# Small retention products for two heads at once on row blocks, S5 outputs in the next input's burst, recurrent units in another order

## The chip, the cores and the metric

The kernel runs on one core of one Trainium2 chip, as one program. The metric is the device time of a run in microseconds (us); a result is the median of several runs. The engines are named as the profile names them: PE is TensorE (its matmuls; PEld are its weight loads), DVE is VectorE, ACT is ScalarE, POOL is GpSimd, SP is SyncE, which only issues DMAs here.

## The reference

One inference step of a two-layer decoder over 560 positions: 528 of a prompt (16 learned meta tokens ahead of 512) and 8 sequences of 4 sampled tokens, which bring their own states. `D_MODEL` is 1024, everything is float32. Each layer:

```
h = rmsnorm(x, g_pre_mix);  z = h @ w_in
u_a, x_b, g_b, q, k, v, g_c, gates = split(z)
y_a = s5_mixer(u_a)          # 48 groups of 16 channels, 64 complex states each;
                             # y = Re(C h) + D u; z = gelu(y); z * sigmoid(z @ w_glu + b)
y_b = rglru_mixer(x_b, g_b)  # width-4 convolution, gated linear recurrence, 768 channels
y_c = retention_mixer(q, k, v, g_c)   # 8 heads, dk 64, dv 128
m = sum of sigmoid(gate_i) * (y_i @ w_branch_i), i = a, b, c
x = x + rmsnorm(m @ w_out, g_post_mix)
h = rmsnorm(x, g_pre_ffn);  gf, uf = split(h @ ffn_w_up)
x = x + rmsnorm((gelu(causal_dwconv(gf)) * uf) @ ffn_w_down, g_post_ffn)
```

Retention works by chunks; for each head

```
scores = einsum('nd,md->nm', q, k) * decay
o      = einsum('nm,me->ne', scores, v) + einsum('nd,de->ne', q, s) * gamma**(n+1)
s_new  = gamma**C * s + einsum('md,me->de', k_dec, v)
```

and `o` is normalized over each head's 128 channels and multiplied by `silu(g_c)`. Outputs are y and the new states of all branches.

## The kernel before

**Columns and weights.** Channels lie on the 128 partitions, positions on the columns: a 1024-channel array is 8 tiles of 128x560, worked on in two halves of 280 columns (`HS`). Weights come in chunks (mostly 128x1024), in the order that `_order` writes out by hand; SP's queue brings each into a raw tile `wr`, ScalarE rounds it to a high part `wh` (fp32r), VectorE subtracts to get the low part `wl`. The same is done with the inputs (`hh`/`hl`, `yh`/`yl`, `fh`/`fl`, `zh`/`zl`). `half` then makes three products for each block of 128 rows, `wh*xh`, `wh*xl` and `wl*xh`, into a PSUM tile `pm`. These weight products are 16128 of TensorE's 19128 instructions. A chunk with 8 blocks is 24 products in each half.

**Small products.** In between stand the mixers' products in plain f32, in bursts, with PSUM tiles `px` (retention, recurrent unit, statistics; two buffers for each tag) and `pz` (S5; one buffer of two banks).

- `s5_gen` runs over n = 0 to 11 (four groups of channels each). For each n a side generator `ahead` makes the unit's weights (`build_B`, `build_C`, `pe_W`, `evac_W`, `build_T`: tiles `Bk`, `br`, `CA`, `Dt`, `W1`, tables `Tc`, `Ts`). Then: the input product (`pz<-V,W`, 16 matmuls on 64x64 tiles), VectorE's rotation and scan into `Hr`, `Hi`, and a step later in the loop `pe_Y(n-1)`: the output product of the unit before (`Hr,CA`, `Hi,CA` on 64x64 tiles, `V,Dt` on the full array), and `evac_Y(n-1)`. `bank(2)` lets only one of these products hold `pz` at a time; `zb` counts. `put_z` writes the outputs z to DRAM (`zd`), and they come back by 24 small loads at the start of the gated unit (`glu`).
- `ret_gen` treats a pair of heads (`hp` = 0 to 3): scores `kf*qf` of 112x112 for each of five chunks (four of the prompt, the fifth of 80 prompt and 32 sampled positions), `sc` by mask; chunk states `S`, a block-diagonal 128x256 tile for two heads; outputs `sc*v` and `S*qf` for both heads into one PSUM tile (`outs`); statistics and normalization; `km`, the sampled positions' keys spread over 8 sequences, times v for the new sample states `ss`; then the outputs are transposed and multiplied into `sg`, the gate's silu, and written to DRAM (`ycd`).

**Order of the work.** A Python planner writes out the program: `Paced` engines keep a model clock `clk`, and `pump`, called after half a unit of weight products, lets the side generators (`start`, `step`) go on when their results should be there and VectorE and ScalarE are not too far ahead (`DEEP`, `SHALLOW`). `finish` runs one to its end. Evacuations of `pm` wait in a list, and `flush` issues them. POOL's queue (`SQ`) takes all DMAs but the weights.

**A layer.** First the products of the u and k columns are made from an input that is not normalized yet. When the sums are there, `normalize` scales the tiles and splits them again, in place (the rewriting: eight `hh` copies and eight `hl` subtractions a half, in the second layer into the tiles named `fh`, `fl`); the products in between, among them v and the first gate `gc`, are scaled column by column with `rn`. Then come k, q, v, gc for each head pair, and between them `LPH` = (1, 1, 2, 2) of the six recurrent units (`xb`, `gb`). After the last pair: `NTC` = 6 of the eight `tc` gate chunks, the retention outputs back from DRAM and split in two (`load_split`, `yh`/`yl`), their projection (`bc`), the recurrent branch's (`tb`, `bb`), S5's gate (`ta`, `glu`) and projection (`ba`), `wo`, and the ConvFFN. In the last layer the halves are 272 and 276 columns.

Of the kernel before, what the change touches and what calls it, by code (L numbers as in the profile page):

```python
# [19 lines left out]
NT = 560  # L20
# [5 lines left out]
C = 112  # L26
MAGIC = 12582912.0
FGRP = (7, 7, 8)
LPH = (1, 1, 2, 2)
NTC = 6  # L30
# [13 lines left out]
_CST = [("ident", 128), ("cos", NT), ("sin", NT), ("causal", C), ("smask", C), ("rowf", 16), ("kdec", 16), ("kds", 64), ("g1", 16), ("g2", 16),  # L44
# [40 lines left out]
def tile_hybrid_decoder(ctx: ExitStack, tc: tile.TileContext, I, O, cfg=None):  # L85
# [123 lines left out]
    kdsT = cc("kds").rearrange("p (h s) -> p h s", h=8)  # L209
# [27 lines left out]
    st = {"raw": 0, "hi": 0, "next": 0, "pool": None, "ahead": 1, "land": 0.0, "paced": False, "shallow": cfg.get("sh0", 1.5), "norm": None}  # L237
# [76 lines left out]
    SLACK, DEEP, SHALLOW = cfg.get("slack", 0.6), cfg.get("deep", 6.0), cfg.get("shallow", 1.0)  # L314
# [27 lines left out]
    def pump():  # L342
# [10 lines left out]
        for s in sorted([s for s in side if not s[4]], key=lambda s: s[2]):  # L353
            if (s in side and s[1] <= clk["P"] and used["n"] + s[3] <= NG
                    and max(clk["V"], clk["A"]) - clk["P"] < (st["shallow"] if s[2] else DEEP)):
                step(s)
# [448 lines left out]
    def s5_gen(l, sp, p, ud, zd, qt):  # L805
# [104 lines left out]
        def pe_Y(n):  # L910
            py = z_ps()
            ca, d = CA[n % 2], Dt[n % 2]
            for j, x in enumerate(X[n]["H"]):
                for a, g, h in QUAD:
                    P.matmul(py[GS[g], a, 0:140], lhsT=ca[j][GS[h], a * 96 + 32:a * 96 + 96], rhs=k3(x)[GS[h], a, 0:140],
                             start=j == 0, stop=False)
            for a in range(2):
                P.matmul(py[:, a, 0:140], lhsT=d[:, a * 128:a * 128 + 128], rhs=V2(n, a), start=False, stop=True)
            X[n]["py"] = py

        def evac_Y(n):
            py = X[n]["py"]
            z = qt("z")
            for a in range(2):
                stt(z[:, a * 140:a * 140 + 140], V2(n, a), vv(l, "s5_d")[:, 2 * n + a:2 * n + a + 1],
                    py[:, a, 0:140], OP.mult, OP.add)
# [42 lines left out]
        for n in range(12):  # L969
# [7 lines left out]
            pz, W1 = z_ps(), x.pop("W1")  # L977
            for j in range(2):
                for a, g, h in QUAD:
                    P.matmul(pz[GS[h], a, j * 140:j * 140 + 140], lhsT=W1[GS[g], a, j * 64:j * 64 + 64], rhs=V2(n, a)[GS[g]],  # L980
                             start=True, stop=True)
# [31 lines left out]
            if n:  # L1013
                evac_Y(n - 1)
                zb["n"] -= 2
# [11 lines left out]
            for j, t in enumerate((hr, hi)):  # L1027
                A.copy(p["fin"][:, j * 24 + a0:j * 24 + a0 + 2], k3(t)[:, :, 140])
        yield 0
        pe_Y(11)  # L1030
# [134 lines left out]
    def ret_gen(l, hp, T, ycd, rp, before):  # L1165
# [77 lines left out]
        yield 2  # L1243
        ss = [slot("ss") for _ in range(2)]
        for h in range(2):
            SQ.dma_start(ss[h][:, :512], I["rets"][l, 2 * hp + h])
        S = rp["S"]
        fin = rp["fin"]
        for h in range(2):
            b = slice(64 * h, 64 * h + 64)  # L1250
            e = slice(h * 128, h * 128 + 128)
            V.tensor_copy(S[0][b, e], p0[b, 0:128])
            for c in range(1, 4):
                stt(S[c][b, e], S[c - 1][b, e], gCT[b, hp, 0:1], p0[b, c * 128:c * 128 + 128], OP.mult, OP.add)
            stt(fin[b, :], S[3][b, e], gCT[b, hp, 1:2], p4[b, :128], OP.mult, OP.add)
# [5 lines left out]
        def outs(c, po):  # L1261
            M = C if c < 4 else 80
            o0 = (c % 2) * 256
            for h in range(2):
                P.matmul(po[:C, o0 + h * 128:o0 + h * 128 + 128],
                         lhsT=(sc[h][:C, c * C:c * C + C] if c < 4 else sc[2][:C, h * C:h * C + C]), rhs=vs(c, h),
                         start=h == 0, stop=c == 0 and h == 1)
            if c:
                P.matmul(po[:M, o0:o0 + 256], lhsT=qf[:, c * C:c * C + M], rhs=S[c - 1], start=False, stop=c < 4)
            if c == 4:  # L1270
                for h in range(2):
                    for s in range(4):
                        P.matmul(po[:C, h * 128:h * 128 + 128], lhsT=qm[h][:, s * C:s * C + C], rhs=ss[h][:, s * 128:s * 128 + 128],
                                 start=False, stop=s == 3 and h == 1)

        def stats(c0, n, po):
            of.append(slot("of"))
            A.copy(of[-1][:C, :n * 256], po[:C, :n * 256])
            for i in range(2 * n):
                V.bn_stats(bn[:C, (c0 * 2 + i) * 6:(c0 * 2 + i) * 6 + 6], po[:C, i * 128:i * 128 + 128])  # L1280

        po, po2 = side_ps(), side_ps()
        outs(0, po)
        outs(1, po)
        outs(2, po2)
        outs(3, po2)
        yield 2
        stats(0, 2, po)
        stats(2, 2, po2)
        yield 0  # L1290
        po = side_ps()
        outs(4, po)
        drop(4)
        yield 3
        stats(4, 1, po)
        km = [slot("km") for _ in range(2)]
# [847 lines left out]
```

## Time and profile before

| | |
|---|---|
| three runs | 2315.74, 2313.77, 2318.67 us; median 2315.74 |
| the profiled execution | 2316.45 us, of which the span is 2314.7 |
| TensorE busy | 2258.6 us, 98% of the span, 19128 matmuls |
| VectorE, ScalarE, POOL busy | 69%, 39%, 14% |
| mean granted clock of TensorE | 0.992 |

The span is the time from the first to the last instruction in the trace, so the execution lies 1.75 us above it. Busy times of engines overlap; a busy TensorE says that a matmul is in it, not that it works at its peak. All instructions are recorded by one helper line (L134), so groups are told apart by their tiles: `pm<-yh,wl` is a product into `pm` of the tiles `yh` and `wl`.

### The profile page before, as it was taken

How to read it: one execution, taken by the hardware profiler on the slowest of the kernel's cores; microseconds unless marked ns; L12 is line 12 of the kernel's file. 1: busy time of each engine (PE TensorE's matmuls, PEld its weight loads, DVE VectorE, ACT ScalarE, POOL GpSimd, SP SyncE). 2: the span in 40 equal slices, each digit the busy share in tenths (PEclk: the TensorE clock that was granted, in tenths of full speed). 3: DMA queues.
4: the chain of work that ended last, by engine and by line, in shares of the span. 5: the costliest groups of instructions: out<-in, count | busy, mean ns of one | idle time of the engine just before them, and what ended most of it. 6: DMA issues, size and time to landing. Idle time of an engine off the chain costs nothing.

```text
span 2314.7 us, 47168 instructions
## 1 busy us (share of the span) xinstructions
PE 2258.6 (98%) x19128; PEld 2217.8 (96%) x19128; DVE 1596.6 (69%) x3817; ACT 906.5 (39%) x1965; POOL 334.1 (14%) x620
## 2 busy tenths in 40 slices
PE   8999999999999999999989999999999999999997
PEld 8999999999999999999989999999999999999996
DVE  7988799885456844546589888898864667364555
ACT  4344446332435433223333445363324354332231
POOL 3231122012010000000243221120111110000011
PEclk9999999999999999999999999999999999999998
DMA  5332333334243232222333332332333432323231
GB/s 177 119 122 82 99 121 103 114 111 121 83 127 126 99 106 86 84 92 83 114 118 100 123 102 92 120 129 87 118 105 95 139 123 96 113 79 95 83 118 46
DMA packets 77146, 245.91 MB, mean 106 GB/s; under 512 B 14272, under 2 KB 17216, under 8 KB 76928
## 3 DMA queue, kind: packets, MB, share of 16 engines
q1 hardware_dynamic: 52704, 175.98, 23.5%
q0 software_dynamic: 24224, 66.92, 9.5%
q8 instruction: 150, 2.46, 0.4%
q14 instruction: 68, 0.56, 0.1%
HBM read 208.23 MB, written 29.76 MB: 103 GB/s over the span
## 4 chain that ended last, share of the span: by engine, by line
PE 71%; DVE 9%; issue 4%; ACT 2%; DMA 2%; POOL 1%; POOLq 0%; DVEq 0%; ACTq 0%
PE pm L134 66%; PE px L134 3%; PE pz L134 2%; DVE wl L134 1%; DVE r L134 1%; ACT wh L134 1%; DMA y<-ycd 1%; DVE part L134 1%; DVE ga L134 1%; DVE sc L134 0%; DVE fo L134 0%; DVE sums L134 0%; POOL out_y L134 0%; DMA wr<-in_wa 0%; DVE cm L134 0%
## 5 line engine op out<-in xcount | busy, mean ns | idle before, releaser
L134 ACT CAST wh<-wr 128x1024 fp32r<-128x1024 f32 (+3 forms) x347 | 346.8, 1004 | 600.8 <-PE pm L134 473.8
L134 DVE TENSOR_TENSOR wl<-wr,wh 128x1024 fp32r<-128x1024 f32 (+3 forms) x347 | 403.6, 1165 | 186.8 <-ACT wh L134 186.5
L134 PE MATMUL pm<-fh,wh 128*128 128x280 f32 (+2 forms) x1632 | 482.1, 295 | 8.3 <-DVE part L134 3.6
L134 PE MATMUL pm<-mh,wh 128*128 128x280 f32 (+2 forms) x1664 | 484.1, 291 | 0.7 <-DVE gp L134 0.7
L134 PE MATMUL pm<-mh,wl 128*128 128x280 f32 (+2 forms) x1664 | 482.6, 290 | 0.0
L134 PE MATMUL pm<-ml,wh 128*128 128x280 f32 (+2 forms) x1664 | 481.9, 290 | 0.0
L134 PE MATMUL pm<-fl,wh 128*128 128x280 f32 (+2 forms) x1632 | 476.6, 292 | 2.7 <-DVE fl L134 2.7
L134 PE MATMUL pm<-fh,wl 128*128 128x280 f32 (+2 forms) x1632 | 475.6, 291 | 0.0
L134 PEld LDWEIGHTS pm<-fh,wh 128*128 128x128 f32 x1632 | 309.5, 190 | 13.4 <-ACT xi L134 3.8
L134 PEld LDWEIGHTS pm<-mh,wh 128*128 128x128 f32 x1664 | 312.8, 188 | 1.6 <-DVE gp L134 1.0
L134 PEld LDWEIGHTS pm<-ml,wh 128*128 128x128 f32 x1664 | 313.3, 188 | 0.3
L134 PEld LDWEIGHTS pm<-mh,wl 128*128 128x128 f32 x1664 | 313.2, 188 | 0.0
L134 PEld LDWEIGHTS pm<-fl,wh 128*128 128x128 f32 x1632 | 309.4, 190 | 3.4 <-DVE fl L134 3.1
L134 PEld LDWEIGHTS pm<-fh,wl 128*128 128x128 f32 x1632 | 309.6, 190 | 0.1
L134 PE MATMUL pm<-hh,wh 128*128 128x280 f32 x928 | 276.8, 298 | 8.5 <-ACT hh L134 6.4
L134 PE MATMUL pm<-hl,wh 128*128 128x280 f32 x928 | 272.5, 294 | 3.3 <-DVE hl L134 3.3
L134 PE MATMUL pm<-hh,wl 128*128 128x280 f32 x928 | 271.6, 293 | 1.0 <-DVE wl L134 1.0
L134 PEld LDWEIGHTS pm<-hh,wh 128*128 128x128 f32 x928 | 175.8, 189 | 12.8 <-ACT hh L134 8.7
L134 PEld LDWEIGHTS pm<-hl,wh 128*128 128x128 f32 x928 | 175.6, 189 | 4.7 <-DVE hl L134 4.5
L134 PEld LDWEIGHTS pm<-hh,wl 128*128 128x128 f32 x928 | 176.2, 190 | 1.3 <-DVE wl L134 1.3
L134 PE MATMUL pm<-yh,wh 128*128 128x280 f32 (+2 forms) x448 | 133.5, 298 | 3.3 <-ACT yh L134 3.3
L134 PE MATMUL pm<-yl,wh 128*128 128x280 f32 (+2 forms) x448 | 131.3, 293 | 0.8 <-DVE yl L134 0.8
(371 smaller groups left out, 4055.4 us busy)
## 6 DMA issues: line engine op xcount, KB each, us to landing
wr<-in_wa SPq DMA_DIRECT2D x249, 512.0 KB, 3.3
wr<-in_w SPq DMA_DIRECT2D x44, 384.0 KB, 3.1
wr<-in_wd SPq DMA_DIRECT2D x32, 448.0 KB, 3.3
wr<-in_wd SPq DMA_DIRECT2D x16, 512.0 KB, 3.6
ycd<-sg POOLq DMA_DIRECT2D x16, 280.0 KB, 3.1
y<-ycd POOLq DMA_DIRECT2D x16, 280.0 KB, 5.6
ss<-in_rets POOLq DMA_DIRECT2D x16, 256.0 KB, 4.2
out_rets<-ss POOLq DMA_DIRECT2D x16, 256.0 KB, 2.6
```

What stands on the lines that cost most here:

```text
L134: return f(out, *a, **k)
```

## The change

Six edits stand in it.

1. **S5.** `pe_Y(n-1)` goes into the same burst and the same `pz` tile as the input product of n (columns 280 to 420 of each bank), ahead of it, with the full-array part `Dt` first. `evac_Y(n-1)` follows VectorE's reading of the input product. Only `pe_Y(11)` stays a burst of its own. The weights of unit n+1 can be built only when the merged burst has read those of n-1.
2. **Retention outputs.** `S` is 128x128, one head on rows 0 to 63, the other on 64 to 127. Each head has its own PSUM tile; `own` makes the eight `sc*v` products of the four prompt chunks, `across` then the six `S*qf` products, on 64 rows each, the heads in turn.
3. **Sample states.** The 32 sampled rows of v and k are brought to rows 0 to 31 and 32 to 63 of a tile `vr` by four small loads on POOL's queue; `km` is built on those 64 rows, and its products use 32 rows each, the heads in turn.
4. **Rewriting.** `normalize` no longer pauses between tiles. The first half is rewritten, all of it at once, between the two halves of the first gate `gc`, the second half right behind them; `DEEP` is lowered to `SHALLOW` (now 2.0) for that stretch.
5. **Order.** `LPH` = (1, 2, 2, 1), `NTC` = 8.
6. **Loads of the retention outputs.** `load_split` keeps up to three loads under way and begins with the heads that are done, before the last pair's `finish`; the last pair's two heads are split straight from `sg`, without DRAM.

```diff
-LPH = (1, 1, 2, 2)
-NTC = 6
+LPH = (1, 2, 2, 1)
+NTC = 8
@@ s5_gen
-        def pe_Y(n):
-            py = z_ps()
+        def pe_Y(n, pz, alone=False):
             ca, d = CA[n % 2], Dt[n % 2]
+            for a in range(2):
+                P.matmul(pz[:, a, 280:420], lhsT=d[:, a * 128:a * 128 + 128], rhs=V2(n, a), start=True, stop=False)
             for j, x in enumerate(X[n]["H"]):
                 for a, g, h in QUAD:
-                    P.matmul(py[GS[g], a, 0:140], lhsT=ca[j][GS[h], a * 96 + 32:a * 96 + 96], rhs=k3(x)[GS[h], a, 0:140],
-                             start=j == 0, stop=False)
-            for a in range(2):
-                P.matmul(py[:, a, 0:140], lhsT=d[:, a * 128:a * 128 + 128], rhs=V2(n, a), start=False, stop=True)
+                    P.matmul(pz[GS[g], a, 280:420], lhsT=ca[j][GS[h], a * 96 + 32:a * 96 + 96], rhs=k3(x)[GS[h], a, 0:140],
+                             start=False, stop=alone and j == 1)
...
             pz, W1 = z_ps(), x.pop("W1")
+            if n:
+                pe_Y(n - 1, pz)
             for j in range(2):
...
+            if n:
+                evac_Y(n - 1)
             zb["n"] -= 2
             yield 0
-            if n:
-                yield from bank(2)
-                pe_Y(n - 1)
-                zb["Y"] = n - 1
...
@@ ret_gen
+        vr = slot("vr")
         for h in range(2):
             SQ.dma_start(ss[h][:, :512], I["rets"][l, 2 * hp + h])
+        for h in range(2):
+            SQ.dma_start(vr[32 * h:32 * h + 32, 0:128], T["v"][2][80:112, h * 128:h * 128 + 128])
+            SQ.dma_start(vr[32 * h:32 * h + 32, 128:192], k4[80:112, h * 64:h * 64 + 64])
...
-            if c:
-                P.matmul(po[:M, o0:o0 + 256], lhsT=qf[:, c * C:c * C + M], rhs=S[c - 1], start=False, stop=c < 4)
...
+                b = slice(64 * h, 64 * h + 64)
+                P.matmul(po[h][:M], lhsT=qf[b, c * C:c * C + M], rhs=S[c - 1][b], start=False, stop=c == 3)
...
+        po = [side_ps(), side_ps()]
+        at = lambda c: [x[:C, c * 128:c * 128 + 128] for x in po]
+        for c in range(4):
+            own(c, at(c))
+        for c in range(1, 4):
+            across(c, at(c))
...
-        for h in range(2):
-            for s in range(4):
-                P.matmul(pn[h][:, s * 128:s * 128 + 128], lhsT=km[h][:C, s * 128:s * 128 + 128], rhs=vs(4, h), start=True, stop=True)
+        for s in range(4):
+            for h in range(2):
+                b = slice(32 * h, 32 * h + 32)
+                P.matmul(pn[h][:, s * 128:s * 128 + 128], lhsT=km[b, s * 128:s * 128 + 128], rhs=vr[b, 0:128], start=True, stop=True)
@@ normalize
             if k:
-                yield 0
                 last()
@@ the layer
-                    halves_apart(us, lambda: finish(normed[1], "norm"))
+                    halves_apart(us, lambda: None)
...
-                    halves_apart(gcs, lambda: free.__setitem__(0, True))
-                    free[1] = True
-                    finish(normed[0], "norm")
+                    def rewrite(h):
+                        free[h] = True
+                        finish(normed[h], "norm")
+                    st["deep"] = SHALLOW
+                    halves_apart(gcs, lambda: rewrite(0))
+                    flush()
+                    rewrite(1)
+                    st["deep"] = DEEP
...
+            yl = start(load_split(ycd[:6], ych, 0.5, lambda i: rets[i // 2] not in side))
             finish(ret, "ret")
-            yl = start(load_split(ycd, ych, 0.5))
             finish(yl, "yl")
+            ych += ych_late
```

How the change moves instructions, at three places. On TensorE, in the retention branch's projection of layer 0, before: an S5 unit's input product (`V,W`), and some 36 weight products further on the output product (`Hr,CA` to `V,Dt`), each between weight products.

```order
L134 MATMUL pm_5509<-yh_5466,wl_5352 128x280
L134 MATMUL pz_5562<-V_5039,W_518_5430 64x140 x8
L134 MATMUL pm_5506<-yh_5472,wh_5245 128x280
...
L134 MATMUL pm_5509<-yh_5484,wl_5352 128x280
L134 MATMUL pz_5629<-Hr_5339,CA_1627 64x140 x4
L134 MATMUL pz_5629<-Hi_5340,CA_1628 64x140 x4
L134 MATMUL pz_5629<-V_3688,Dt_1630 128x140 x2
L134 MATMUL pm_5506<-yh_5490,wh_5245 128x280
```

After, in the same projection:

```order
L134 MATMUL pm_5752<-yh_5290,wl_5563 128x280
L134 MATMUL pz_5782<-V_4377,Dt_1758 128x140 x2
L134 MATMUL pz_5782<-Hr_5624,CA_1755 64x140 x4
L134 MATMUL pz_5782<-Hi_5625,CA_1756 64x140 x4
L134 MATMUL pz_5782<-V_5373,W_549_5669 64x140 x8
L134 MATMUL pm_5801<-yh_5532,wh_5562 128x280
```

Two bursts became one, in one `pz` tile, and the full-array part moved to its head. (Each row here is a matmul as the program has it; the trace records two for each f32 matmul.)

On TensorE, at the first head pair of layer 0, the outputs of the prompt's chunks; before, the heads' `sc*v` in one PSUM tile for two chunks, each chunk followed by one product with the block-diagonal `S`:

```order
L134 MATMUL px_1608<-v_1005,sc_1354 112x128
L134 MATMUL px_1608<-v_1005,sc_1355 112x128
L134 MATMUL px_1608<-S_822,qf_894 112x256
L134 MATMUL px_1609<-v_1083,sc_1354 112x128
L134 MATMUL px_1609<-v_1083,sc_1355 112x128
L134 MATMUL px_1609<-S_823,qf_894 112x256
```

After, with a PSUM tile for each head:

```order
L134 MATMUL px_1715<-v_1079,sc_1473 112x128
L134 MATMUL px_1716<-v_1079,sc_1474 112x128
L134 MATMUL px_1715<-S_822,qf_890 112x128
L134 MATMUL px_1716<-S_822,qf_890 112x128
L134 MATMUL px_1715<-S_823,qf_890 112x128
L134 MATMUL px_1716<-S_823,qf_890 112x128
L134 MATMUL px_1715<-S_824,qf_890 112x128
L134 MATMUL px_1716<-S_824,qf_890 112x128
```

All eight products with `sc` (the last two are shown) come first now, and six half-wide products with `S` stand together behind them, alternating between the heads.

On VectorE, at the rewriting of layer 0, before: `hl` is the rewritten low part, `pm` and `sg` the evacuation of the first gate, `tBr`, `tBi` an S5 table, `kd` retention.

```order
L134 TENSOR_TENSOR hl_143<-x_71,hh_142 128x280
L134 TENSOR_TENSOR pm_1202<-pm_1202,rn_110 128x280
L134 SCALAR_TENSOR_TENSOR sg_1167<-sg_1167,pm_1202 128x280
L134 TENSOR_TENSOR tBr_1229<-tBr_1229,sc_56_516 128x24x2
...
L134 TENSOR_TENSOR tBi_1230<-tBi_1230,bt_513 128x24x2
L134 TENSOR_TENSOR wl_1242<-wr_1111,wh_1241 128x1024
L134 TENSOR_TENSOR hl_147<-x_72,hh_146 128x280
L134 TENSOR_TENSOR kd_1283<-px_1191,cst 112x512
L134 TENSOR_TENSOR kd_819<-px_1192,cst 112x128
L134 TENSOR_TENSOR hl_154<-x_73,hh_153 128x280
```

After:

```order
L134 SCALAR_TENSOR_TENSOR sg_1183<-sg_1183,pm_1150 128x280
L134 TENSOR_TENSOR hl_143<-x_71,hh_142 128x280
L134 TENSOR_TENSOR hl_147<-x_72,hh_146 128x280
L134 TENSOR_TENSOR hl_154<-x_73,hh_153 128x280
...
L134 TENSOR_TENSOR hl_177<-x_78,hh_176 128x280
L134 TENSOR_TENSOR pm_1203<-pm_1203,rn_110 128x280
L134 SCALAR_TENSOR_TENSOR sg_1163<-sg_1163,pm_1203 128x280
L134 TENSOR_TENSOR wl_1229<-wr_1107,wh_1228 128x1024
```

The eight subtractions of the first half stand in a row, directly behind the gate's evacuation of that half; the table, the weight conversion and `kd` are elsewhere.

## Rows read from the trace of the kernel before

**Rows 1.** The page: engines' busy time, and the chain that ended last.
```profile
PE 2258.6 (98%) x19128; PEld 2217.8 (96%) x19128; DVE 1596.6 (69%) x3817; ACT 906.5 (39%) x1965; POOL 334.1 (14%) x620
...
PE 71%; DVE 9%; issue 4%; ACT 2%; DMA 2%; POOL 1%; POOLq 0%; DVEq 0%; ACTq 0%
```

**Rows 2.** Timeline of PE, an S5 output: start us, us, instruction.
```profile
508.77 0.29 PE L134 MATMUL pm<-yl,wh 128*128 128x280 f32 x1
508.90 0.29 PE L134 MATMUL pm<-yh,wl 128*128 128x280 f32 x1
509.12 0.47 PE L134 MATMUL pz<-Hr,CA 64*64 64x140 f32 x8
509.41 0.42 PE L134 MATMUL pz<-Hi,CA 64*64 64x140 f32 x8
509.76 0.74 PE L134 MATMUL pz<-V,Dt 128*128 128x140 f32 x4
510.25 0.38 PE L134 MATMUL pm<-yh,wh 128*128 128x280 f32 x1
```

**Rows 3.** Waits of PE, whole span: us in total, times, longest us.
```profile
PE pz L134 <- DVE hn L134: 4.6, 4, 2.1
...
PE pm L134 <- DVE hl L134: 3.3, 3, 2.5
PE pm L134 <- ACT yh L134: 3.3, 2, 2.2
PE pm L134 <- DVE fl L134: 2.7, 2, 2.4
```

**Rows 4.** Windows: us, busy (x) PE, PEld, DVE, ACT, POOL; PEclk, DMA, GB/s.
```profile
96.00:100.00 4.00, 3.72 (x24) 3.26 (x25) 3.54 (x9) 0.43 (x2) 0.00 (x0) 0.57 0.27 109
1253.00:1260.00 7.00, 6.10 (x26) 5.64 (x27) 6.46 (x23) 2.15 (x7) 0.00 (x0) 0.53 0.45 150
```

**Rows 5.** Timeline of PE, an S5 input.
```profile
412.29 0.29 PE L134 MATMUL pm<-yh,wl 128*128 128x280 f32 x1
412.51 0.71 PE L134 MATMUL pz<-V,W 64*64 64x140 f32 x16
413.15 0.40 PE L134 MATMUL pm<-yh,wh 128*128 128x280 f32 x1
```

**Rows 6.** Timeline of PE, retention outputs of the four prompt chunks.
```profile
349.25 0.29 PE L134 MATMUL pm<-hh,wl 128*128 128x280 f32 x1
349.38 1.04 PE L134 MATMUL px<-v,sc 112*112 112x128 f32 x8
350.25 0.60 PE L134 MATMUL px<-S,qf 128*112 128x256 f32 x2
...
352.24 0.48 PE L134 MATMUL pm<-hh,wh 128*128 128x280 f32 x1
```

**Rows 7.** Timeline of PE, scores of two heads.
```profile
248.42 0.29 PE L134 MATMUL pm<-hh,wl 128*128 128x280 f32 x1
248.64 1.04 PE L134 MATMUL px<-qf,kf 64*112 64x112 f32 x16
249.61 0.40 PE L134 MATMUL pm<-hh,wh 128*128 128x280 f32 x1
```

**Rows 8.** Timeline of PE, the sample states' update.
```profile
212.09 0.28 PE L134 MATMUL pm<-wh,hl 128*112 128x256 f32 x1
212.21 1.95 PE L134 MATMUL px<-v,km 112*128 112x128 f32 x16
213.91 0.37 PE L134 MATMUL pm<-wh,hh 128*112 128x256 f32 x1
```

**Rows 9.** Timeline of DVE, six subtractions of the rewriting.
```profile
95.78 2.24 DVE L134 TENSOR_TENSOR hl<-x,hh 128x280 fp32r<-128x280 f32 x6
```

**Rows 10.** Timeline, layer 1: PE's last S5 output; POOL's loads of z behind it.
```profile
1723.03 0.47 PE L134 MATMUL pz<-Hr,CA 64*64 64x140 f32 x8
...
1735.10 8.13 POOL L134 DMA_DIRECT2D z<-zd  x15 [0.98 <-DMA z<-zd]
```

**Rows 11.** DMA issues, 1728 to 1750 us: KB each, median us to landing.
```profile
z<-zd POOLq DMA_DIRECT2D x24, 70.0 KB, 3.5
```

More of the change, by code (lines that the diff above doesn't have):

```diff
@@ L236, in tile_hybrid_decoder @@
     live, liveX = set(), set()
-    st = {"raw": 0, "hi": 0, "next": 0, "pool": None, "ahead": 1, "land": 0.0, "paced": False, "shallow": cfg.get("sh0", 1.5), "norm": None}
+    st = {"raw": 0, "hi": 0, "next": 0, "pool": None, "ahead": 1, "land": 0.0, "paced": False, "shallow": cfg.get("sh0", 1.5), "norm": None, "deep": cfg.get("deep", 6.0)}
     BOOT = cfg.get("boot", 3)
@@ L1028, in s5_gen @@
                 A.copy(p["fin"][:, j * 24 + a0:j * 24 + a0 + 2], k3(t)[:, :, 140])
+        yield from bank(2)
         yield 0
-        pe_Y(11)
+        pe_Y(11, z_ps(), True)
         yield 0
@@ L1162, in lru_gen, with ret_gen @@
         drop()
-    def ret_gen(l, hp, T, ycd, rp, before):
+    def ret_gen(l, hp, T, ycd, rp, before, straight=None):
         kf, qf = T["k"], T["q"]
@@ L1259, in ret_gen, with o_of, own, across @@
         of = []
-        def outs(c, po):
+        def o_of(c, h):
+            return of[h][:C, c * 128:c * 128 + 128] if c < 4 else of[2][:C, h * 128:h * 128 + 128]
+        def own(c, po):
+            for h in range(2):
+                P.matmul(po[h], lhsT=(sc[h][:C, c * C:c * C + C] if c < 4 else sc[2][:C, h * C:h * C + C]), rhs=vs(c, h),
+                         start=c % 4 == 0, stop=False)
+        def across(c, po):
             M = C if c < 4 else 80
-            o0 = (c % 2) * 256
@@ new lines, in stats @@
+        def stats(c, h, ps):
+            i = c * 2 + h
+            V.bn_stats(bn[:C, i * 6:i * 6 + 6], ps)
+        po = [side_ps(), side_ps()]
+        at = lambda c: [x[:C, c * 128:c * 128 + 128] for x in po]
+        for c in range(4):
+            own(c, at(c))
+        for c in range(1, 4):
+            across(c, at(c))
+        yield 2
+        for h in range(2):
+            of.append(slot("of"))
+            A.copy(of[h][:C, :512], po[h][:C, :512])
+            for c in range(4):
+                stats(c, h, at(c)[h])
@@ new lines, in ret_gen @@
+        yield 0
+        po = [side_ps(), side_ps()]
+        own(4, at(0))
+        across(4, at(0))
+        for s in range(4):
+            for h in range(2):
+                P.matmul(po[h][:C, :128], lhsT=qm[h][:, s * C:s * C + C], rhs=ss[h][:, s * 128:s * 128 + 128],
+                         start=False, stop=s == 3)
+        drop(4)
+        yield 2
+        of.append(slot("of"))
+        for h in range(2):
+            A.copy(o_of(4, h), po[h][:C, :128])
+            stats(4, h, po[h][:C, :128])
@@ L1348, in ret_gen @@
             stt(sg[:, 448:560], pb[:, :112], g, sg[:, 448:560], OP.mult, OP.mult)
-            yield 0
-            SQ.dma_start(ycd[hd], sg)
-            drop()
+            if straight is None:
+                yield 0
+                SQ.dma_start(ycd[hd], sg)
+                drop()
+            else:
+                yield 2
+                a, b = slot("yh", FR), slot("yl", FR)
+                split(sg, a, b, ALL, 0.5)
+                drop()
+                straight.append((a, b))
         drop(3)
@@ L1549, in tile_hybrid_decoder @@
                       fin=sp.tile([128, 128], FT, name=f"fin{l}"),
-                      S=[sp.tile([128, 256], FT, name=f"S{l}{c}") for c in range(4)],
+                      S=[sp.tile([128, 128], FT, name=f"S{l}{c}") for c in range(4)],
                       bn=sp.tile([128, 60], FT, name=f"bn{l}"), mv=sp.tile([128, 20], FT, name=f"mv{l}"),
                       rn=sp.tile([128, 10], FT, name=f"rn{l}"), nb=sp.tile([128, 10], FT, name=f"nb{l}"))
-            for t in rp["qm"] + rp["S"]:
+            for t in rp["qm"]:
                 G.memset(t, 0.0)
@@ L1597, in tile_hybrid_decoder @@
                 flush()
[L1598 removed]
+                ret = start(ret_gen(l, hp, T, ycd, rp, ret, ych_late if hp == 3 else None))
+                rets.append(ret)
                 T["v"] = []
@@ L1666, in gate, with load_split @@
                 return box
-            def load_split(srcs, out, scale=None):
-                for src in srcs:
-                    yield 3
-                    t = slot("y")
-                    SQ.dma_start(t, src)
+            def load_split(srcs, out, scale=None, there=lambda i: True):
+                on, i = [], 0
+                while on or i < len(srcs):
+                    while i < len(srcs) and len(on) < 3 and there(i) and used["n"] + 3 <= NG:
+                        on.append((slot("y"), clk["P"] + 4.5))
+                        SQ.dma_start(on[-1][0], srcs[i])
+                        i += 1
+                    if not on or clk["P"] < on[0][1]:
+                        yield 0 if on else 3
+                        continue
                     yield 2
+                    t = on.pop(0)[0]
                     a, b = slot("yh", FR), slot("yl", FR)
@@ L2080, in _pack @@
     kd = np.zeros((C, 2, 8))
-    kds = np.zeros((C, 8, 8))
+    kdr = np.zeros((64, 4, 8))
     g1 = np.zeros((C, 2, 8))
```

73 lines of the change are left out of this document (22 added, 51 removed).

## The prediction

> **What bounds the kernel now.** I read the page first, then TensorE's waits, then its timeline around the small products. TensorE has work on it for 98% of the span, and it carries 71% of the chain that ended last [rows 1]. So time can come from three places only: fewer or denser matmuls, waits in front of a matmul, and stretches at the half clock. The weight products are untouched by the change. In the timeline a following one starts 0.13 us after the one before (508.77 to 508.90), whatever its "busy" time of 0.29 says, since they overlap [rows 2]. What the change touches are the small f32 products, which run in bursts between the weight products. A burst's price is the distance from the last weight product before it to the first one after it, less that 0.13.
>
> The waits that bear on the change are short: 3.3 us for hl and 2.7 us for fl (the rewriting of the split input in layers 0 and 1, where fl holds it), 4.6 us for hn (the output product of a recurrent unit of the S5 branch waits until VectorE has read its input product out of the same PSUM buffer), and 3.3 us for yh (the first product of the retention branch's projection) [rows 3]. The first two are dearer than they look: right behind them the granted clock averages 0.57 over 4 us and 0.53 over 7 us [rows 4], stretches at the lower of its two levels, 1.2 instead of 2.4 GHz.
>
> **The change part by part.**
>
> *S5 outputs in the next input's burst.* Before, a unit's output product is a burst of its own: 510.25 - 508.90 - 0.13 = 1.22 us [rows 2]. Its next input product is another: 413.15 - 412.29 - 0.13 = 0.73 us [rows 5]. The second is 16 records on 64x64 tiles, four side by side. 140 columns in two passes at 2.4 GHz are 0.117 us, so four rounds are 0.47 and 0.26 us is left for entering and leaving the small tiles. The first has four such rounds and four records of the full array (Dt), 0.94 together, and 0.28 left. Merged, with Dt ahead while the array is still whole, it is twelve times 0.117 plus one such rest: 1.40 + 0.27 = 1.67 instead of 1.95. The program has 22 such pairs (11 in each layer; the last output of each stays alone): 22 x 0.28 = 6.2 us.
>
> *Retention outputs by row blocks.* Before, the four prompt chunks cost 352.24 - 349.25 - 0.13 = 2.86 us. The first eight sc records take 350.25 - 349.38 = 0.87, 0.109 each, so 16 are 1.74 and the products with the state S 1.12 [rows 6]. S was block diagonal, half of it zeros, 256 columns on 128 rows; now it is 128 columns on 64 rows for each head. No such product is in the trace; the nearest is the score product, two heads in two row blocks and two PSUM banks: eight of 112 columns cost 249.61 - 248.42 - 0.13 = 1.06 us [rows 7]. Four passes of 112 columns would be 0.187 each if they ran one after the other, 1.49 for eight, more than the whole burst; two at a time they are 0.75 with 0.31 left for entering and leaving. Six of 128 columns are then 6 x 0.107 + 0.31 = 0.95, and the burst 2.69: 0.17 less, eight times (four pairs of heads, two layers), 1.4 us. The sample chunk has one such product, 1.12 / 3 = 0.37; two of half the width take 0.21 + 0.31 = 0.52, since the products around them stay on the whole array. That is 0.15 lost, eight times: +1.2.
>
> *Sample state update.* km times v: 16 records on 112 rows, 213.91 - 212.09 - 0.12 = 1.70 us, which is 16 x 0.107 with nothing left over [rows 8]. Now 32 rows for each head, two heads side by side: 0.85 + 0.31 = 1.16, again by [rows 7] since no product on 32 rows is in the trace. 0.54 less, eight times: 4.3 us. The bounds are one after the other (8 x 0.213 + 0.31 = 2.01, so 2.5 us lost) and no rest at all (0.85, 6.8 us won). I take the middle one because its only difference from [rows 7] is the block's height. The four small transfers that fetch these rows go out on POOL's queue right behind the state's load, several bursts ahead of km; POOL is busy 14% [rows 1], and I price them at nothing, or some tenths for the first head pair if they landed late.
>
> Here a rule speaks against the change. In the trace a burst that stays on the whole array has no rest [rows 8], one on smaller tiles has 0.26 to 0.31 [rows 5, 7], and the change makes 24 retention bursts pay it once. The Trainium skill's page "TensorEngine Tiling (Array Packing)", section Key Properties, says that changing the tiling mode drains the engine; the trace agrees, with that rest as its price, which the page doesn't give. By that rule alone the 24 would lose 24 x 0.31 = 7.4 us; with the halved streaming, as above, they win 1.4 - 1.2 + 4.3 = 4.5.
>
> Together: -6.2 - 1.4 + 1.2 - 4.3 = -10.7 us of TensorE work.
>
> *The rewriting.* Before, VectorE reaches the second subtraction of the first half only behind table products, a weight conversion and retention work, and TensorE, which is already at the recurrent unit, waits. The last six take 2.24 us in a row, 0.37 each, once they are let through [rows 9]. After, all eight of a half stand together, directly behind the gate's evacuation, and the program puts them under the 48 weight products of the gate's second half (48 x 0.13 = 6.2 us): 8 x 0.37 = 3.0 us fits. The second half sits under the recurrent unit's first halves in the same way. What goes is 3.3 + 2.7 us of waits [rows 3] and 4.0 x 0.43 + 7.0 x 0.47 = 5.0 us of lost clock [rows 4]: 11.0. A conversion of the next weight is now behind the eight, so I leave 1 us standing: -10.
>
> *The other waits.* The merged burst no longer waits for hn, but it waits for the later of the unit's state and the next unit's weights; I keep half of the 4.6: -2.3. For yh I count nothing: the loads start earlier and two heads skip DRAM, but ScalarE still does the last gate's tanh and then the first split, and VectorE the rest, before the projection may begin. The loads were not all of it, and the stall of 3.3 is the bound.
>
> *What is late next.* The S5 chain of a unit now has two bursts instead of three, but the output waits for the next input, so the chain is longer per unit; in layer 0 the program puts the last output 60 weight products before the branch's end, where it stood 357 before. Behind it 24 loads on POOL's queue bring z back. In layer 1 of the trace that takes from 1723.03 until the last issue ends at 1735.10 + 8.13 = 1743.23, and 3.5 us to land: 23.7 us [rows 10, 11]. In layer 0 after, the GLU starts 156 weight products and a burst after that output (20.3 + 1.2 = 21.5 us) and wants the sixth tile 15 products later, at 23.4; it is there at 23.7 plus its split in two (two 560-wide steps at twice 0.37, by [rows 9]): 1.5 us late, estimate. I take +1.3, between none and 3.
>
> *Sum.* -10.7 - 10 - 2.3 + 1.3 = -21.7. The profiled execution took 2316.45 us, 1.75 more than its span and 0.7 above the median shown: 2316.45 - 21.7 = 2294.75, or 2294 against the median.
>
> **Rivals.**
> A. *Row blocks don't run side by side*: km is at +2.5 instead of -4.3, and S gives 6 x 0.213 + 0.31 = 1.59, +3.8 instead of -1.4. 12 us dearer: 2306. Against it stands [rows 7]; for it only that no 32-row product is in the trace. (The page's rule alone comes to the same: 7.4 lost instead of 4.5 won.)
> B. *The waits come back elsewhere.* VectorE is busy 69% over the span [rows 1]; work put off by the rewriting (score masks, tables) is late a few us afterwards, and at the start of the projection six splits stand in its queue ahead of the state that the next merged burst needs. Then the 12.3 us of saved waits return: 2306, up to 2310 with a lower clock behind them.
> C. *Slower: every merged burst waits.* TensorE runs in order, so a burst that waits for Hi holds up all weight products. Four of 24 output bursts waited for hn, 4.6 us in all [rows 3]. From (21.7 + 4.6) / 22 = 1.2 us of wait in each the kernel would be slower by 0.2%; at 1.5 us it is 2327. Against it: 20 of the 24 didn't wait before, though their inputs came from the same VectorE queue.
> D. *No gain at all*: VectorE, not TensorE, sets the pace of the mixers, and what TensorE saves it waits: 2312 to 2318. Against it: TensorE's named waits are far below its 98%.
>
> **How the numbers follow.** Forecast 0.61 (its own range 2284 to 2302), A 0.08, B 0.19, D 0.07, C 0.05. The low end is all waits gone and no rests: -10.7 - 11 - 4.6 - 3.3 = -29.6, and the 2.5 us by which km's lower bound lies under the value taken, -32: 2284; two more stretches of half clock, behind the waits for yh and hn, would give back 3.4 if those waits go (each like that of layer 0's rewriting): 2280. The high end takes in A and B: 2310. Faster by over 0.2% (4.6 us, about what a measurement of this kernel can tell from no change): forecast, A and B, 0.88; same 0.07; slower 0.05.
>
> **What would show it.** Right: merged bursts of about 1.67 us, km bursts of 1.16, four-chunk bursts of 2.69; no wait for hl or fl and no stretch of half clock at 96 and 1253 us; about 1 us of wait for zh or zl in layer 0 alone. Wrong: km bursts near 2.0 (A), waits for Hi, CA or yl of over 10 us in all (B, C), or bursts as priced but a span that doesn't follow (D).

## The result, and the profile after

The changed kernel takes 2287.60 us, the median of four runs (2285.52 to 2289.62), against 2317.03 for the kernel before in the same session (2313.77 to 2318.67): 29.4 us less, ratio 0.9872 with a 95% interval of 0.9860 to 0.9884. The prediction was 2294 (2280 to 2310). The profiled execution is the longest of the four: 2289.62 us, span 2287.8, so the two profiles lie 26.9 us apart.

The page after, engines' busy time and the chain that ended last [rows 1]:

```profile
PE 2241.0 (98%) x19192; PEld 2205.4 (96%) x19192; DVE 1574.4 (69%) x3769; ACT 903.0 (39%) x1972; POOL 341.2 (15%) x636
...
PE 83%; DVE 7%; issue 5%; ACT 2%; DMA 1%; POOL 1%; SPq 0%; POOLq 0%; DVEq 0%; ACTq 0%
```

TensorE has 64 matmul records more and 17.6 us less busy time. VectorE has 48 instructions and 22 us less, which the prediction didn't list: the state updates of two heads are one instruction on 128 partitions now, where they were two on 64, and `km` is one product of 64 rows where it was two of 112. These steps make 18 of the 22 us.

Waits of PE after (us in total, times, longest), the rows that answer to [rows 3] and what is new:

```profile
PE pz L134 <- DVE CA L134: 3.5, 4, 1.8
PE pm L134 <- ACT yh L134: 3.5, 2, 2.4
...
PE pz L134 <- DVE Hi L134: 1.4, 2, 1.2
...
PE pm L134 <- DVE yl L134: 0.8, 2, 0.4
...
PE pm L134 <- DVE zl L134: 0.2, 1, 0.2
```

No wait for hl, fl or hn is left. The wait for yh stands as it was (3.3 before). New are CA and Hi, 4.9 us together: the weights and the state for which TensorE now waits (Hi holds up a merged burst, CA the burst that makes a unit's weights).

Windows after at the places of [rows 4] (us; busy of PE, PEld, DVE, ACT, POOL; granted clock, DMA share, GB/s), and at the start of the branch projection:

```profile
92.00:100.00 8.00, 8.00 (x65) 8.00 (x65) 7.06 (x18) 6.71 (x19) 1.05 (x2) 1.00 0.28 97
1237.00:1244.00 7.00, 6.58 (x51) 6.09 (x50) 6.53 (x18) 4.32 (x13) 0.00 (x0) 1.00 0.22 76
404.00:412.00 8.00, 5.19 (x38) 4.75 (x37) 7.35 (x18) 6.06 (x17) 1.06 (x2) 1.00 0.09 18
```

Both stretches of the rewriting run at the full clock, with TensorE busy for 8.0 of 8 and 6.6 of 7 us. One stretch of half clock is new: behind the wait for CA at 1611 us in layer 1 the clock is 0.83 over 1606 to 1616 us. On VectorE each half's eight subtractions stand in a row, as [rows 9] had six:

```profile
91.15 2.96 DVE L134 TENSOR_TENSOR hl<-x,hh 128x280 fp32r<-128x280 f32 x8
...
97.73 2.96 DVE L134 TENSOR_TENSOR hl<-x,hh 128x280 fp32r<-128x280 f32 x8
```

The bursts after, in PE's timeline (start us, us): a merged S5 burst, `km`, and the four prompt chunks, each from the last weight product ahead to the first one behind.

```profile
400.94 0.29 PE L134 MATMUL pm<-hh,wl 128*128 128x280 f32 x1
401.07 0.64 PE L134 MATMUL pz<-V,Dt 128*128 128x140 f32 x4
401.64 0.47 PE L134 MATMUL pz<-Hr,CA 64*64 64x140 f32 x8
401.93 0.42 PE L134 MATMUL pz<-Hi,CA 64*64 64x140 f32 x8
402.16 0.66 PE L134 MATMUL pz<-V,W 64*64 64x140 f32 x16
402.75 0.40 PE L134 MATMUL pm<-hh,wh 128*128 128x280 f32 x1
```

```profile
144.02 0.29 PE L134 MATMUL pm<-hh,wl 128*128 128x280 f32 x1
144.24 1.16 PE L134 MATMUL px<-vr,km 32*128 32x128 f32 x16
145.33 0.39 PE L134 MATMUL pm<-hh,wh 128*128 128x280 f32 x1
```

```profile
193.12 0.29 PE L134 MATMUL pm<-hh,wl 128*128 128x280 f32 x1
193.24 1.91 PE L134 MATMUL px<-v,sc 112*112 112x128 f32 x16
195.08 0.91 PE L134 MATMUL px<-S,qf 64*112 64x128 f32 x12
195.92 0.40 PE L134 MATMUL pm<-hh,wh 128*128 128x280 f32 x1
```

So 402.75 - 400.94 - 0.13 = 1.68 (1.95 for the two bursts before), 1.18 (1.70 before [rows 8]) and 2.67 (2.86 before [rows 6]).

To see where the time went, each trace was worked through like this. A weight product should start 0.129 us after the one before it (0.127, 0.125 and 0.118 for 276, 272 and 256 columns); what it starts later is a stall, lost clock included. A burst counts with the price of its kind without a wait, and what it takes beyond that is a stall too. The figures are of one execution of each kernel, the profiled one. By place, over both layers, in us (rewriting: 85 to 112 and 1215 to 1262; head pairs: from there to 385 and 1505; branch projection: on to 515 and 1665; z: around 590 and 1740):

| kernel | bursts | rewriting | head pairs | projection | z |
|---|---|---|---|---|---|
| before | 167.9 | 12.7 | 8.2 | 22.8 | 0 |
| changed | 157.3 | 1.4 | 6.7 | 15.6 | 0.4 |
| difference | -10.6 | -11.3 | -1.5 | -7.2 | +0.4 |

Together -30.2. The rest of the program, which no edit touches, is 3.4 us longer in this profile (in all fourteen profiles of this study it lies within 6.5 us), which leaves -26.8, against 26.9 between the spans.

### The profile page after: what moved, and what is told of

Same layout as the page of the kernel before. It is cut to its first block, busy times and chain, and to the rows that moved or that the text cites. A ratio compares the mean times of both kernels' runs of the same rounds, so it can differ in the third digit from the quotient of the medians.

```text
span 2287.8 us, 47360 instructions
## 1 busy us (share of the span) xinstructions
PE 2241.0 (98%) x19192; PEld 2205.4 (96%) x19192; DVE 1574.4 (69%) x3769; ACT 903.0 (39%) x1972; POOL 341.2 (15%) x636
## 4 chain that ended last, share of the span: by engine, by line
PE 83%; DVE 7%; issue 5%; ACT 2%; DMA 1%; POOL 1%; SPq 0%; POOLq 0%; DVEq 0%; ACTq 0%
PE pm L134 77%; PE px L134 4%; PE pz L134 2%; DVE wl L134 1%; DVE part L134 1%; ACT wh L134 1%; DVE fo L134 1%; DVE sc L134 0%; DMA wr<-in_wa 0%; DVE sums L134 0%; POOL out_y L134 0%; DVE yl L134 0%; DMA z<-zd 0%; POOL z L134 0%; DVE fl L134 0%
```

## The experiments

No edit was expected to need another, so the first runs had one edit each, on the kernel before; the loads (edit 6) were not run alone. Medians are set against the kernel before in the same session (2317.0 to 2318.1).

**One edit alone.** S5, retention (`S`, prompt chunks, `km`), rewriting, and the two lines of numbers: the hunks of the diff above, each set by itself (a line or two of each is shown; the retention edit takes its changed points of pause for the planner with it).

```diff
@@ only_s5
+            if n:
+                pe_Y(n - 1, pz)
@@ only_ret
+                P.matmul(po[h][:M], lhsT=qf[b, c * C:c * C + M], rhs=S[c - 1][b], start=False, stop=c == 3)
@@ only_rewrite
+                    halves_apart(gcs, lambda: rewrite(0))
@@ only_order
+LPH = (1, 2, 2, 1)
+NTC = 8
```

> The kernel before with the S5 edit alone. Theory 1 (TensorE is the bound, so a shorter burst shows in the time in full): merged bursts at 1.67 us give 6.0 us, and the waits for hn (4.6 us) and the half clock behind one of them go with it, less 2 us of new waits for Hi and CA: 6 to 9 us faster, about 2309. Rival (VectorE sets the pace in the mixers, the saved time comes back as waits): bursts at the same price, but TensorE's waits up by as much, no change, 2315 to 2319.

> The kernel before with the row blocks of retention alone (S, the four prompt chunks, km; yields as in the changed kernel). Theory 1: prompt bursts 2.86 to 2.68, sample chunk 2.54 to 2.66, km 1.70 to 1.18, eight of each, together 4.6 us faster, 2312.5, and no wait of before goes. Rival 1 (VectorE sets the pace): no change. Rival 2 (the order of the work, which the planner now writes otherwise, decides): anything from 4 us slower to 10 us faster, with waits in the trace that differ by as much.

> The kernel before with the rewriting alone. Theory 1: the waits for hl and fl and the two half-clock stretches go (5.8 us around 90 to 110 us, 6.0 us around 1250), nothing else: 11 us faster, 2306. Rival (VectorE's other work is late instead): the two places are clean, but waits of 3 to 10 us stand 10 to 100 us later, in the masks, tables or the branch projection: 2309 to 2316.

> The kernel before with the two lines of numbers alone (LPH and NTC). Theory 1: no work is removed, and waits at the start of the branch projection shrink a little: within 4 us of before, 2313 to 2319. Rival 2 (the order gives the 6 us by which the change was better than forecast): the waits between 390 and 425 us and between 1520 and 1650 us fall from 19 us to 12, so 7 us faster, 2310.

| alone | median | ratio (95%) | bursts | rewriting | head pairs | projection |
|---|---|---|---|---|---|---|
| only_s5 | 2312.22, -5.8 | 0.9974 (0.9965 to 0.9982) | 162.1 | 11.8 | 7.2 | 24.0 |
| only_ret | 2331.21, +13.2 | 1.0065 (1.0051 to 1.0078) | 162.9 | 10.2 | 9.8 | 37.7 |
| only_rewrite | 2322.45, +4.4 | 1.0023 (1.0014 to 1.0032) | 167.8 | 3.3 | 8.1 | 35.4 |
| only_order | 2318.01, 0.0 | 1.0004 (0.9995 to 1.0013) | 168.0 | 12.3 | 11.7 | 20.1 |

The first three edits did at their own places about what they were priced at: bursts -5.8 and -5.0, rewriting -9.4. The times followed only in only_s5, just short of its theory's 6 to 9 us, and there in part by luck: the waits for hn went, but those for yh grew from 3.3 to 7.8 us. only_order stayed where its theory 1 had it, and its rival's 7 us did not come. only_ret and only_rewrite became slower than any of their expectations allowed: retention alone lost 14.9 us at the projection, and the rewriting alone 12.6. Waits of PE in only_ret:

```profile
PE pm L134 <- ACT yh L134: 7.8, 3, 4.7
...
PE pz L134 <- DVE hn L134: 6.5, 3, 3.8
PE pz L134 <- DVE z L134: 5.3, 2, 3.2
PE pm L134 <- DVE tg L134: 3.6, 1, 3.6
```

and in only_rewrite:

```profile
PE pz L134 <- DVE z L134: 7.3, 4, 3.2
...
PE pz L134 <- DVE hn L134: 5.7, 3, 3.9
PE pm L134 <- ACT yh L134: 5.2, 2, 4.0
```

The same three stand in both: yh, hn, and z (a unit's weight burst waits until VectorE has read the output product out of the single `pz` tile). The waits for yh, and some of those for z, are at the start of the projection, where TensorE meets VectorE's backlog. The other waits for z and most of those for hn come towards its end (489 to 501 and 1645 to 1653 us). POOL's timeline in only_ret shows how a late z goes on: POOL stands idle for 12.34 us until z is there to be written, and the last head's write and the loads for yh stand behind it.

```profile
398.89 1.07 POOL L134 DMA_DIRECT2D zd<-z  x2 [12.34 <-ACT z L134]
399.94 0.56 POOL L134 DMA_DIRECT2D ycd<-sg  x1
400.50 3.19 POOL L134 DMA_DIRECT2D y<-ycd  x6
405.52 0.54 POOL L134 DMA_DIRECT2D y<-ycd  x1 [1.83 <-DMA zd<-z]
```

My theory 1, that a shorter burst shows in the time in full, holds for S5 alone. For retention and the rewriting the time came back as waits, as the rivals had it, and more came back than was saved.

**One edit left out.** The same hunks, each taken back from the changed kernel, and the loads too.

```diff
@@ no_s5
-                pe_Y(n - 1, pz)
@@ no_ret
-                P.matmul(po[h][:M], lhsT=qf[b, c * C:c * C + M], rhs=S[c - 1][b], start=False, stop=c == 3)
@@ no_rewrite
-                    halves_apart(gcs, lambda: rewrite(0))
@@ no_order
-LPH = (1, 2, 2, 1)
-NTC = 8
@@ no_loads
-            yl = start(load_split(ycd[:6], ych, 0.5, lambda i: rets[i // 2] not in side))
+            yl = start(load_split(ycd, ych, 0.5))
```

> The changed kernel with the S5 edit taken back (output and input bursts apart as before). After the first four runs, in which three edits alone gave nothing or cost time: theory 1, the edits' bursts are paid as priced and the waits depend on how much VectorE has queued where the branch projection begins; without the S5 edit 6 us of bursts come back and hn waits of 2 to 5 us: 2296 to 2299. Rival (the parts only gain together, since any one of them tips the planner's order): 2305 or more.

> The changed kernel with the row blocks of retention taken back. Theory 1: bursts of retention cost 4.6 us more, and VectorE has the state updates of two heads apart again (some 20 us of its work): 4.6 us plus 3 to 8 us of waits, 2295 to 2300. Rival (the row blocks cost time, as alone): not slower than the changed kernel, 2275 to 2288.

> The changed kernel with the rewriting taken back. Theory 1: the two stretches at 90 to 110 us and around 1250 us come back, 11 us: 2298. Rival (VectorE's work is only moved, as in the run of that edit alone, where 11 us gained there came back later): 2285 to 2291.

> The changed kernel with the old numbers of LPH and NTC. Theory 1: the waits for yh at the start of the branch projection grow, since two recurrent units stand behind the last head pair and two gate chunks less: 3 to 8 us slower, 2291 to 2295. Rival 2 (order is worth nothing, as alone): 2286 to 2290. Rival (the order is what lets the other edits gain): 2300 or more.

> The changed kernel with the old loads of the retention outputs: all eight heads written to DRAM, read back one after another once the last pair is finished. Theory 1 (the projection's start hangs on POOL's queue, where these loads stand behind the last write of a head and a write of z that waits for VectorE; in the run of retention alone that made waits of 5 us for yh): waits for yh and yl of 7 to 12 us over both layers instead of 4.3, the kernel 4 to 9 us slower, 2292 to 2297. Rival (ScalarE's splits behind the last gate are the limit, not the loads): waits as in the changed kernel, 2286 to 2290.

| left out | median, against before | ratio (95%) | bursts | rewriting | head pairs | projection | z |
|---|---|---|---|---|---|---|---|
| (none) | 2287.60, -29.4 | 0.9872 (0.9860 to 0.9884) | 157.3 | 1.4 | 6.7 | 15.6 | 0.4 |
| no_s5 | 2303.30, -14.8 | 0.9938 (0.9926 to 0.9951) | 163.2 | 4.5 | 6.4 | 22.6 | 0 |
| no_ret | 2295.06, -23.1 | 0.9901 (0.9886 to 0.9917) | 161.8 | 3.8 | 7.5 | 12.6 | 1.8 |
| no_rewrite | 2296.10, -22.0 | 0.9905 (0.9892 to 0.9919) | 157.3 | 9.6 | 8.3 | 12.6 | 0 |
| no_order | 2295.04, -23.1 | 0.9900 (0.9887 to 0.9914) | 157.6 | 1.6 | 10.3 | 18.1 | 0 |
| no_loads | 2297.69, -20.0 | 0.9914 (0.9899 to 0.9929) | 157.3 | 3.0 | 6.7 | 22.8 | 1.0 |

Each of the five is worth 6 to 15 us inside the whole, the three that were worth nothing or less alone too: retention 6, rewriting 7, order 6, loads 9, S5 15 (its bursts are 5.9 of that); by the intervals each is uncertain by some 4 us. The five sum to 44, more than the whole. So the edits overlap, and a worth also holds what the planner's new order costs when an edit is taken back. In no_s5 a single input burst waits 6.8 us for Dt at 480 us, a wait that stands neither before nor after:

```profile
PE pz L134 <- ACT Dt L134: 6.8, 1, 6.8
```

No wait for hn came back there, and the time lies between theory 1 and the rival. no_ret has theory 1's time, but not its waits: at the projection it stalls 3.0 us less than the changed kernel (its profiled execution is its fastest, 2290.53 us). In no_rewrite 8.2 of the 11.3 us came back, and the time lies between theory 1 and the rival. no_order is as theory 1 had it, with the waits for yh up from 3.5 to 5.5 us. no_loads came out just above the 2297 that theory 1 gave at most, but not by its mechanism: the waits for yh did not grow, they fell from 3.5 to 2.1. What grew is CA:

```profile
PE pz L134 <- DVE CA L134: 8.7, 6, 3.5
```

The timelines of VectorE and POOL there, in layer 0:

```profile
405.31 4.66 DVE L134 SCALAR_TENSOR_TENSOR yl<-y,yh 128x560 fp32r<-128x560 f32 x7 [0.70 <-ACT yh L134]
411.05 0.74 DVE L134 SCALAR_TENSOR_TENSOR yl<-y,yh 128x560 fp32r<-128x560 f32 x1 [1.08 <-ACT yh L134]
...
414.33 0.29 DVE L134 TENSOR_TENSOR CA<-cm,cm 128x128 f32<-128x128 f32 x1
```

```profile
407.00 0.54 POOL L134 DMA_DIRECT2D y<-ycd  x1 [11.79 <-DVE yl L134]
```

The eighth split waits for its load (the eighth y could only be fetched when the first was split), and the first of the weights CA of the next S5 unit stands behind it in VectorE's queue until 414.33 + 0.29 = 414.62; the weight burst waits 3.5 us for it. In layer 1 a wait of 3.2 us stands in the same way behind the six splits of the recurrent branch's outputs, which the same generator loads. So the loads' price is paid behind the place where I looked for it.

**Row blocks head by head.** The changed kernel; the same products in another order.

```diff
-        for s in range(4):
-            for h in range(2):
+        for h in range(2):
+            for s in range(4):
                 b = slice(32 * h, 32 * h + 32)
                 P.matmul(pn[h][:, s * 128:s * 128 + 128], lhsT=km[b, s * 128:s * 128 + 128], rhs=vr[b, 0:128], start=True, stop=True)
```

and the six products with `S` likewise.

> The changed kernel with the products of km and of the chunk state issued head by head (four and three of one head, then of the other) and nothing else altered. Theory 1 (two row blocks stream side by side only if neighbours in the program are of different heads): a km burst of 8 x 0.213 + 0.31 = 2.0 us instead of 1.18, a prompt burst of 3.3 instead of 2.68, together 11.7 us slower, 2299. Rival (the gain is from something else, such as half the rows or another PSUM bank): bursts at 1.18 and 2.68, 2286 to 2290.

It takes 2295.28 us, -22.4 against before, ratio 0.9908 (0.9891 to 0.9924): 7.0 slower than the changed kernel. PE's timeline around `km`:

```profile
144.29 0.29 PE L134 MATMUL pm<-hh,wl 128*128 128x280 f32 x1
144.51 1.71 PE L134 MATMUL px<-vr,km 32*128 32x128 f32 x16
146.15 0.40 PE L134 MATMUL pm<-hh,wh 128*128 128x280 f32 x1
```

and around the prompt chunks:

```profile
193.93 0.29 PE L134 MATMUL pm<-hh,wl 128*128 128x280 f32 x1
194.05 1.91 PE L134 MATMUL px<-v,sc 112*112 112x128 f32 x16
195.89 1.22 PE L134 MATMUL px<-S,qf 64*112 64x128 f32 x12
197.04 0.40 PE L134 MATMUL pm<-hh,wh 128*128 128x280 f32 x1
```

1.73 against 1.18, and 2.98 against 2.67: eight times 0.55 and 0.31 is 6.9 us. That the medians differ by nearly the same is in part luck: they are uncertain by some 4 us, and the two profiled spans differ by 4.3 (2292.1 against 2287.8). The order in the program decides whether the two heads stream side by side; that is theory 1. Its price was wrong: 1.73 is 16 x 0.107 = 1.71 and 0.02, not 2.0, and 2.98 less 1.74 for `sc` is 1.24, less than 12 x 0.107 = 1.28. Head by head there is no rest at all.

Neighbours of different heads differ in two things, the row block and the PSUM tile. Another PSUM tile alone does not do it: the sixteen `sc` records alternate theirs on 112 rows, and 195.08 - 193.24 = 1.84 us are 0.115 for each. Whether two row blocks would also stream side by side into one PSUM tile was not run.

**Going on from the changed kernel.** The splits of the retention outputs start after five of the eight gate chunks; and then also three sets of S5 output weights.

```diff
-            box = [gate("tc") for _ in range(NTC)]
-            flush()
+            box = [gate("tc") for _ in range(5)]
             yl = start(load_split(ycd[:6], ych, 0.5, lambda i: rets[i // 2] not in side))
+            box += [gate("tc") for _ in range(5, NTC)]
+            flush()
```

```diff
-            ca, d = CA[n % 2], Dt[n % 2]
+            ca, d = CA[n % 3], Dt[n % 3]
...
-                while zb["Y"] < n - 2:
+                while zb["Y"] < n - 3:
```

> A version that goes on from the changed kernel: the generator that loads and splits the retention outputs starts after the fifth of the eight gate chunks, not after the eighth, so three of its six splits stand ahead of the last gate's evacuation in ScalarE's queue. Theory 1 (what is left of the wait for yh is the order in ScalarE's queue): the waits for yh and yl (4.3 us over both layers) fall under 1 us, and the wait for CA behind the six yl in layer 0 (1.4 us) with them: 2282 to 2284. Rival (VectorE and ScalarE are full there, the splits only push the S5 work): waits for Hi, CA and Dt up by as much, 2286 to 2290.

> As the version before, and three sets of the S5 output weights (CA, Dt) instead of two, so that a unit's weights can be built before the merged burst has read those of two units earlier. Theory 1 (the merged burst lengthened the chain from one unit to the next, and the waits for CA are its price): waits for CA (3.5 us in the changed kernel) fall under 1 us, 2279 to 2283. Rival (they come from VectorE's queue, not from the buffer): as the version before, 2282 to 2284.

The first takes 2286.39 us (-31.3 against before, ratio 0.9866, 0.9851 to 0.9881), which isn't told apart from the changed kernel. Its waits for yh and yl are gone (a wait of 1.1 us for tg stands at that product in layer 1), CA is at 2.4 us, and the projection's stalls fall from 15.6 to 9.9. So theory 1 was right about the waits and not about the time, and the rival the other way round. But a wait for z takes their place in layer 0:

```profile
PE pm L134 <- ACT zh L134: 2.6, 1, 2.6
PE pz L134 <- DVE CA L134: 2.4, 2, 2.0
```

with its window (582 to 594 us) at the lower clock for part of the time:

```profile
582.00:594.00 12.00, 8.67 (x51) 7.96 (x50) 5.10 (x7) 3.67 (x9) 2.73 (x6) 0.86 0.41 108
```

Stalls at z rise from 0.4 to 5.6, about what was won. TensorE reaches the first product with z at 583.6 us, 6.5 earlier than in the changed kernel, but POOL's loads of z end at 584.7 us, only 3.7 earlier:

```profile
579.87 4.86 POOL L134 DMA_DIRECT2D z<-zd  x9 [0.28 <-DMA z<-zd]
```

So in layer 0 the S5 chain with its way through DRAM is what comes next. The second takes 2289.66 us (ratio 0.9883, 0.9868 to 0.9897), no better: CA waits 2.2 us, so the two sets were not the limit. The rival (VectorE's queue) holds: in VectorE's timeline CA stands behind the splits of the recurrent branch's outputs in layer 1.

```profile
1603.94 3.34 DVE L134 TENSOR_TENSOR yl<-y,yh 128x560 fp32r<-128x560 f32 x5
...
1609.68 0.29 DVE L134 TENSOR_TENSOR CA<-cm,cm 128x128 f32<-128x128 f32 x1
```

No version that is measurably faster than the changed kernel was found.

## Why the prediction was right, point by point

*Small products.* Forecast -10.7, measured -10.6: merged bursts 1.67 forecast and 1.68 measured, prompt chunks 2.69 and 2.67, the sample chunk 0.15 dearer and 0.13 measured (2.54 to 2.67), `km` 1.16 and 1.18. Pricing [rows 7] over to 64 and 32 rows held, and rival A is shown to be wrong, with the alternation of the heads as the reason.

*What the rest is.* Here a step failed, though its sum held. The prediction put the rest of 0.26 to 0.31 us down to entering and leaving the smaller tiles. Head by head the tiles are entered and left just the same, and the rest is 0.02 or less. In these rows it comes only with two blocks side by side: 1.18 - 8 x 0.107 = 0.32 for eight pairs, 2.67 - 1.74 - 6 x 0.107 = 0.29 for six, [rows 7] 0.31 for eight. The sample chunk, with two pairs, has 0.37 + 0.13 - 0.21 = 0.29. So it doesn't grow with the number of pairs. The bound "one after the other" was 0.3 too high for the same reason. The rule that I weighed (the Trainium skill, "TensorEngine Tiling (Array Packing)", Key Properties: changing the mode drains the engine) shows no price of its own in these rows; whether some overlap at the change from one head to the other hides it, they don't tell.

*The rewriting.* Forecast -10, measured -11.3: both waits and both half-clock stretches went. That it loses by itself (+4.4) was not foreseen; rival B had the mechanism, but with no more lost than saved.

*The other waits.* This is the mis-sized term, and its mechanism failed: -2.3 forecast, -7.2 at the projection and -1.5 at the head pairs measured. It kept half of the wait for hn as new waits. All of hn went (4.6), and CA and Hi brought 4.9, so this exchange gained nothing. For yh nothing was counted, and the wait itself did not change (3.3 and 3.5). The gain is what had no term. Of waits before, these stood at the projection and are gone after:

```profile
PE pz L134 <- DVE z L134: 2.3, 2, 1.3
PE pm L134 <- DVE tg L134: 1.5, 1, 1.5
```

So are one of 0.9 us for xc and one of 0.7 for ScalarE's tg. The half clock behind the waits at 405 and 420 us, which only the low end of the range had counted, went as well; one stretch came back at 1611 us. Order and loads were counted at nothing and are worth 6 and 9 us inside the whole. Why these waits went was not isolated, so that the sum of -21.7 came near the measured -29.4 is luck in this part. VectorE's 22 us less of work had no term either; what they are worth was not measured by itself.

*What is late next.* z: +1.3 forecast, +0.4 measured, of which 0.2 is a wait for zl in layer 0. The last step of its sum has a slip: 23.7 and two steps of 0.74 are 25.2, which is 1.8 after 23.4 and not 1.5. The place was right, and early_split shows it: 5.7 us won at the projection, 5.2 lost at z.

*Rivals.* B (waits come back) is wrong for the whole and right for two of its parts. C: the merged bursts wait 1.4 us for Hi in all, far from 1.2 us each. D: the span fell by 26.9 us, so TensorE's savings were not waited away.

*What stays open.* In only_ret and only_rewrite VectorE is late at the projection, and the traces show who waits for it; which steps the planner put ahead there was not isolated, since every edit makes it write the whole order anew. For the same reason the 7.2 us at the projection are not divided among the edits. Of what remains after, the waits for yh, CA and z give way to each other, as no_loads and early_split show.

## What to carry to other kernels

Here small products on row blocks gained only when neighbours in the program used different blocks (and PSUM tiles); check a burst's price with the blocks in turn. An edit that is priced correctly at its own place can lose more where an engine's backlog meets the next stage: when a planner writes the order, take the sum from the whole and test edits by leaving them out, not only by doing them alone. Look at the trace even so, since leaving one out also brings a new order. Before hastening a stage's start, look at what the stage after it waits for.

## What was not expected of the hardware

The side-by-side price is a fixed 0.3 us for a group of pairs, and none for the same tiles in turn (above). And a wait of nearly the same length does not always bring the lower clock. Before, TensorE waited 2.2 us for yh until 405.5 us, and 0.9 us for a burst some six us earlier; the window around it in the kernel before has the clock (the third number from the end) at 0.83:

```profile
402.00:412.00 10.00, 7.37 (x43) 6.94 (x43) 5.76 (x10) 5.27 (x9) 3.59 (x7) 0.83 0.92 312
```

After, it waited 2.4 us until 407.0, and the clock stayed at 1.00 (the window from 404 to 412 above). In early_split waits of 0.4 and 2.6 us, three us apart, brought 0.86. From these three a shorter wait ahead of the long one would seem to decide. It does not: no_ret waited 2.4 us for yh until 408.2, with no other wait of over 0.3 us in the ten us ahead, and over the same window as after its clock is 0.79.

```profile
404.00:412.00 8.00, 5.19 (x30) 4.76 (x27) 7.21 (x20) 5.68 (x15) 1.06 (x2) 0.79 0.09 20
```

What decides, these rows don't tell.
